# Attention scores on one Trainium2 core: the turned part as two fp32r products with split queries

## The chip, the cores and the metric

The kernel runs on one core of a Trainium2 chip. The metric is the time of one execution on the device in microseconds (us). A core has a matrix engine (TensorE, "PE" in the profile, with its weight loads as "PEld"), three engines for elementwise work (VectorE "DVE", ScalarE "ACT", GpSimd "POOL"), a SyncE queue ("SP") that starts transfers here, an on-chip memory SBUF of 128 partitions, and PSUM, into whose banks TensorE writes its products. Each engine works through a queue of its own and waits for others by semaphores.

## The reference

The program is a two-layer trunk over 256 positions of width 1024. Each layer is a feed-forward part, a mixer and another feed-forward part; the first layer's mixer is a convolution module, the second's is latent attention with 8 heads. The change touches the scores of that attention alone:

```python
q_nope, q_rope = q[..., :QK_NOPE], q[..., QK_NOPE:]          # 128 and 64 wide
q_rope = apply_rope(q_rope, cos[:, :, None, :], sin[:, :, None, :])
k_rope = apply_rope(k_rope, cos, sin)                         # one key for all heads
...
s = (jnp.einsum("bqhd,bkhd->bhqk", q_nope[:, q0:q1], k_nope[:, :q1],
                preferred_element_type=jnp.float32)
     + jnp.einsum("bqhr,bkr->bhqk", q_rope[:, q0:q1], k_rope[:, :q1],
                  preferred_element_type=jnp.float32)) * scale
mask = chunk_id[q0:q1, None] >= chunk_id[None, :q1]
s = jnp.where(mask[None, None], s, -jnp.inf)
p = jax.nn.softmax(s, axis=-1).astype(v.dtype)
outs.append(jnp.einsum("bhqk,bkhd->bqhd", p, v[:, :q1]))
```

Queries go in two blocks of 128; block 0 sees 128 keys, block 1 all 256. Within a block the mask lets a query see the chunks of 64 positions up to its own.

## The kernel before

**Number formats.** TensorE multiplies tiles declared fp32 in two recorded instructions per matmul and tiles declared fp32r (a rounded fp32) in one. Nearly all weight products of the kernel are therefore split: a weight is cast on ScalarE to an fp32r high part `hi` (L246), VectorE subtracts to get the low part `lo` (L247), and three fp32r products (`mm3`, L332, L335, L336) take the place of one fp32 product. Inside the attention, the scores and the value products are plain fp32.

**Where the scores get their operands.** `nope` (its eviction is L1522) projects the unturned queries `QN` and keys `KN`. The turned ("rope") queries of a block of 128 positions come as `qr`, are turned by VectorE in `rope` (L1407 to L1414, with scratch tiles of tag `rp512`), transposed on TensorE (L443, tile `tp`) four pairs of heads at a time, and copied out of PSUM into `QR` (recorded as L258, since the helper `urgent` wraps the call): the even heads, lying in partitions 0 to 63, by ScalarE, the odd heads, in partitions 64 to 127, by VectorE. `QR` has room for both parities, 128 partitions each; the 64 partitions that a parity doesn't use hold zeros and two rows of ones. `KR`, the turned key, is laid out the same way (L1554): the key in the half of its parity, and -1e30 in the two rows of the other half that meet the ones, which is how the mask is added by the product itself. GpSimd fills these constants at the start of the attention (L1432, L1437). The turned key is transposed with both halves alike, so each half of the 128 partitions holds the whole 64-wide key.

**The scores.** For each head `scores` takes one PSUM bank and, for both query blocks, adds an fp32 product of `QN` and `KN` (L1581) and one of `QR` and `KR` (L1582). `softmax` takes row maxima on VectorE (L1594, scaled in L1595), exponentials on ScalarE (L1597), reciprocal and scaling on VectorE (L1600, L1602). The probabilities are transposed (L443), copied by ScalarE (`ptT`, L1609), multiplied with the values `VV` (L1618, L1619), and the output is split by ScalarE and VectorE (L1613, L1614) for the output projection.

**Order.** Heads 0, 1 and 2 are scored first, then the unturned queries of the last four heads are projected (48 matmuls), then heads 3 to 7 follow one by one with the output projection's products between them. The values are projected (`v`, evicted in L1569 to `VV`) between the transposes of the queries and the first scores. Before the first exponential ScalarE loads its table, with a dummy exponential placed behind the last eviction of `VV`. A scheduler at build time settles the order in each engine's queue from priorities (`urgent` raises one) and from explicit `order` calls; on the chip the queues run as written. PSUM tiles of tag "B" share three banks in rotation: the transposed keys of the two blocks, the transposed queries of the two blocks and then the scores of heads 0, 1, 2 take them one after the other. A tile waits until the readers of the tile before it in the same bank are done.

Of the kernel before, what the change touches and what calls it, by code (L numbers as in the profile page):

```python
# [11 lines left out]
F32 = mybir.dt.float32  # L12
F32R = mybir.dt.float32r
# [6 lines left out]
P = 128  # L20
D = 1024
S = 256
# [5 lines left out]
CHUNK = 64  # L28
# [3 lines left out]
H = 8  # L32
# [57 lines left out]
def trunk(ctx: ExitStack, tc: tile.TileContext, x, xt, first, pos, invf, gfin, wdw,  # L90
          f1w13, f1w2, f2w13, f2w2, cw1, cw2, wa, wuq, wukv, wo, wpair, out):
    nc = tc.nc
# [12 lines left out]
    def uid(s):  # L105
        n_uid[0] += 1
        return f"{s}_{n_uid[0]}"
# [4 lines left out]
    def bank(tag, name):  # L112
        return ps.tile([P, 512], F32, tag=tag, name=uid(name), bufs=BANKS[tag])
# [40 lines left out]
    def order(ins, first):  # L154
        tc.add_manual_dep(ins.ins, first.name, mybir.DependencyInfo(
            mybir.DependencyClass.NoSync, mybir.DependencyReason.DATA), reason="order")
# [95 lines left out]
    def urgent(f):  # L252

        def g(*args, **kw):
            traced = nc.cur_bb.bb.instructions
            n = len(traced)
            with tc.high_priority():
                r = f(*args, **kw)  # L258
            last = {ins.engine: ins for ins in traced[n:]}
            for engine, ins in last.items():  # L260
                ahead_of.setdefault(engine, []).append(ins)
            return r
        return g
# [8 lines left out]
    def weights(n=1, more=True):  # L272
        out = []
        for _ in range(n):
            n_used[0] += 1
            if more:
                load_ahead()
            else:
                load_ahead(0)
            out.append(loaded[n_used[0] - 1])  # L280
        return out
# [48 lines left out]
    def mm3(o, ah, al, bh, bl, start, stop, after=(), seeded=False):  # L330

        mm = nc.tensor.matmul(o, ah, bl, start=start, stop=False, skip_group_check=seeded)  # L332
        for a in after:
            order(mm, a.ins)
        nc.tensor.matmul(o, ah, bh, start=False, stop=False, skip_group_check=seeded)  # L335
        return nc.tensor.matmul(o, al, bh, start=False, stop=stop, skip_group_check=seeded)  # L336
# [75 lines left out]
    def tbs(tb):  # L412
        return slice(tb * P, (tb + 1) * P)
# [26 lines left out]
    def transposed(src, q, n, after=(), turned=None):  # L440
        b = bank("B", "tp")
        for j in range(n):
            tp = nc.tensor.transpose(b[:, j * P:(j + 1) * P], src[:, (q + j) * P:(q + j + 1) * P], ident)  # L443
            if turned is not None:
                turned.append(tp)
            for a in after:
                order(tp, a.ins)
        return b
# [951 lines left out]
    def rope(pool, dst, src, n, cc, sn, tb, after=()):  # L1400

        w = n * 64
        t1, t2 = (pool.tile([P, w], F32, tag=f"rp{w}", name=uid("rp"), bufs=3 if n > 1 else 4) for _ in range(2))
        a = t1[:, :w].rearrange("p (n i f) -> p n i f", i=2, f=32)
        b = t2[:, :w].rearrange("p (n i f) -> p n i f", i=2, f=32)
        full = [P, n, 2, 32]
        turned = [nc.vector.tensor_tensor(a, src, cc[:, tb, :, :].unsqueeze(1).to_broadcast(full), op=ALU.mult)]  # L1407
        for i in range(2):
            turned.append(nc.vector.tensor_tensor(b[:, :, i, :], src[:, :, 1 - i, :],
                                                  sn[:, tb, i, :].unsqueeze(1).to_broadcast([P, n, 32]), op=ALU.mult))  # L1410
        for ins in turned:
            for first in after:
                order(ins, first.ins)
        nc.vector.tensor_add(dst, t1[:, :w], t2[:, :w])  # L1414


    def mla(X, make_next, cc, sn):
        with tc.tile_pool(name="mla", bufs=1) as act:
            return mla_in(act, X, make_next, cc, sn)

    def mla_in(act, X, make_next, cc, sn):
# [4 lines left out]
        CKl = act.tile([P, 2, S], F32R, tag="CKl", name="CKl")  # L1426


        KR = act.tile([P, 2, S], F32, tag="KR", name="KR")
        QR = act.tile([P, 2, H // 2, S], F32, tag="QR", name="QR")  # L1430
        for x, fill in ((KR, -1e30), (QR, 1.0)):
            nc.gpsimd.memset(x, 0.0)  # L1432
            for parity in range(2):
                for tb in range(NT):
                    row = 64 * (1 - parity) + 32 * tb
                    t = tb * P + (CHUNK if x is KR else 0)
                    nc.gpsimd.memset(x[row:row + 1, parity, ..., t:t + CHUNK], fill)  # L1437

        last_low = [None]

# [42 lines left out]
        last = None  # L1483
        for tb in range(NT):
# [5 lines left out]
            last = last_low[0]  # L1490
# [17 lines left out]
        KN = xp.tile([P, H, S], F32, tag="Xh", name="KN")  # L1508
        QN = xp.tile([P, H, S], F32, tag="Xl", name="QN")
        VV = act.tile([P, NT, H * VH], F32, tag="VV", name="VV")  # L1510

        def nope(part, dst, nk, ch, cl, width, h0, heads, after=()):

            hi, lo = part
            for i in range(heads[0], heads[1], 2):
                b = bank("A", "nope")
                for e in range(2):
                    for k in range(nk):
                        c = slice(k * width + (i + e) * P, k * width + (i + e + 1) * P)
                        mm = mm3(b[:, e * S:(e + 1) * S], hi[:, c], lo[:, c], ch[:, k, :], cl[:, k, :],  # L1520
                                 k == 0, k == nk - 1, after if k == 0 else ())
                nc.scalar.copy(dst[:, h0 + i:h0 + i + 2, :], b.rearrange("p (e t) -> p e t", t=S))  # L1522
            return mm
# [4 lines left out]
        for tb in range(NT):  # L1528
            u = bank("A", "qr")
            qu.append(u)  # L1530
            for k in range(4):
                after = (last,) if k == 0 else turned if (tb, k) == (0, 2) else ()
                last = mm3(u, CQh[:, k, tbs(tb)], CQl[:, k, tbs(tb)], hi[:, k * 512:(k + 1) * 512],
                           lo[:, k * 512:(k + 1) * 512], k == 0, k == 3, after)
# [14 lines left out]
        last = nope(part, QN, 4, CQh, CQl, 512, 0, (0, 4), turned)  # L1549
        for t in range(NT):  # L1550
            b = transposed(kd[t], 0, 1, (last,))
            for i in range(2):
                half = slice(64 * i, 64 * i + 64)
                nc.scalar.copy(KR[half, i, tbs(t)], b[half, :P])  # L1554
        for tb in range(NT):
            b = transposed(qr[tb], 0, 4, (last,)).rearrange("p (j t) -> p j t", t=P)
            for parity, copy in ((0, nc.scalar.copy), (1, nc.vector.tensor_copy)):
                half = slice(64 * parity, 64 * parity + 64)
                urgent(copy)(QR[half, parity, :, tbs(tb)], b[half])
        kpart, = weights()  # L1560
        nope(kpart, KN, 2, CKh, CKl, D, 0, (0, H))
        (hi, lo), = weights()
        for tb in range(NT):
            for d in range(2):
                b = bank("A", "v")
# [10 lines left out]
        def scores(hd):  # L1576
            b = bank("B", "sc")
            sc = {0: b[:, :P], 1: b[:, P:P + S]}
            for qb in range(NT):
                n = (qb + 1) * P  # L1580
                nc.tensor.matmul(sc[qb], QN[:, hd, tbs(qb)], KN[:, hd, :n], start=True, stop=False)  # L1581
                last = nc.tensor.matmul(sc[qb], QR[:, hd % 2, hd // 2, tbs(qb)], KR[:, hd % 2, :n], start=False,  # L1582
                                        stop=True)
            score_last.append(last)
            return softmax(sc)

        @urgent
        def softmax(sc):
            nm = small.tile([P, NT], F32, tag="nm", name=uid("nm"))
            sm = small.tile([P, NT], F32, tag="sm", name=uid("sm"))  # L1590
            pr = act.tile([P, 3 * P], F32, tag="pr", name=uid("pr"), bufs=3)
            pn = {0: pr[:, :P], 1: pr[:, P:]}
            for qb in range(NT):
                nc.vector.reduce_max(nm[:, qb:qb + 1], sc[qb], axis=AX.X)  # L1594
            maxima.append(nc.vector.tensor_scalar(nm, nm, -SCALE, None, op0=ALU.mult))  # L1595
            for qb in range(NT):
                last = nc.scalar.activation(pn[qb], sc[qb], AF.Exp, scale=SCALE, bias=nm[:, qb:qb + 1],  # L1597
                                            accum_out=sm[:, qb:qb + 1])
            powers.append(last)
            nc.vector.reciprocal(sm, sm)  # L1600
            for qb in range(NT):
                last = nc.vector.tensor_scalar(pn[qb], pn[qb], sm[:, qb:qb + 1], None, op0=ALU.mult)  # L1602
            scaled.append(last)
            return pr
# [22 lines left out]
        table = urgent(nc.scalar.activation)(small.tile([P, 1], F32, tag="silu", name="exp"), neghalf, AF.Exp)  # L1627
        order(table, kept.ins)
        pr[0] = scores(0)
        pr[1] = scores(1)  # L1630
        pr[2] = scores(2)

        for j, i, highs, lows in ((0, 0, None, maxima[2]), (0, 1, None, scaled[0]), (1, 0, powers[2], scaled[1]),
# [51 lines left out]
    class Rows512:  # L1685

        n = {"ht": 0, "hb": 0}
# [128 lines left out]
```

## Time and profile before

| | |
|---|---|
| runs | 896.81, 897.5, 900.43 us (median 897.5) |
| the profiled execution | 897.52 us, of which the span 895.7 us |
| TensorE busy | 887.9 us (99% of the span) |
| VectorE busy | 743.6 us (83%) |
| ScalarE busy | 571.8 us (64%) |
| attention, first scores to last output product | about 667 to 714 us of the span |
| score products (L1581, L1582) | 32 records each: 8 heads, 2 blocks, 2 records per fp32 matmul |

How to read the profile: times are from the span's start. In the timeline a row is start, duration, engine, line, operation, output<-inputs, shape and count; in brackets stands the idle time of the engine before it and what ended that. Consecutive equal instructions are merged into one row ("x4"). A TensorE record's duration includes the pipeline's fill and drain, so neighbouring records overlap and the cost of a matmul is read from start to start. The profile prints fp32r operands of TensorE as f32; which they are follows from the tiles. In the chain of waits a row is start, length, engine, tile and line of a piece of the chain that ended last.

### The profile page before, as it was taken

To read this page: it belongs to the slowest core of one execution; us is meant where nothing else is said; L and a number is where in the kernel's file an instruction comes from. 1 tells how busy PE (TensorE), PEld (TensorE's weight loads), DVE (VectorE), ACT (ScalarE), POOL (GpSimd) and SP (SyncE) were. 2 spreads that over 40 slices of the span, in tenths; PEclk is the share of its full clock that TensorE was granted. 3 is DMA by queue.
4 is the path that set the end of the run, shared out by engine and by line. 5 is a ranking of instruction groups with operands and counts; after the bars stand their busy time and mean duration, and the time that the engine had idled before them with its cause. 6 is when DMAs were issued, how large, how long until landed. Compare 5 with 4: busy or idle time off the path is not lost.

```text
span 895.7 us, 12244 instructions
## 1 busy us (share of the span) xinstructions
PE 887.9 (99%) x4221; PEld 745.7 (83%) x4221; DVE 743.6 (83%) x1083; ACT 571.8 (64%) x993; POOL 105.2 (12%) x227
## 2 busy tenths in 40 slices
PE   9999999999999999999999999999999999999997
PEld 7888888898988888888888888888899888888886
DVE  6787779579998999999598989995768579999973
ACT  7966458488876646656375566673677566474762
POOL 1000000079962000000010000001400010000000
PEclk9999999999999999999999999999999999999999
DMA  9997629834215864939759369396635449387551
GB/s 336 354 341 252 229 59 367 296 124 165 95 60 193 291 257 147 386 97 372 271 177 340 113 221 350 114 387 202 219 142 189 141 147 345 107 285 291 165 210 48
DMA packets 71054, 198.94 MB, mean 222 GB/s; under 512 B 12368, under 2 KB 41936, under 8 KB 51664
## 3 DMA queue, kind: packets, MB, share of 16 engines
q1 hardware_dynamic: 70560, 197.47, 61.9%
q8 instruction: 33, 0.54, 0.2%
q10 hardware_dynamic: 432, 0.69, 0.2%
q14 instruction: 29, 0.24, 0.1%
HBM read 181.87 MB, written 16.25 MB: 221 GB/s over the span
## 4 chain that ended last, share of the span: by engine, by line
PE 78%; DVE 10%; DMA 8%; issue 2%; SPq 1%; ACT 1%; POOL 0%; DVEq 0%; ACTq 0%
PE u L332 10%; PE u L336 10%; PE u L335 10%; PE o L336 9%; PE o L332 9%; PE o L335 9%; PE u L1002 3%; PE gate L1002 3%; DVE lo L247 3%; DMA gd<-gt 2%; PE u L408 2%; DVE lo L200 2%; DMA raw<-in_f2w 1%; DMA rows<-gd 1%; DMA hd<-rows 1%
## 5 line engine op out<-in xcount | busy, mean ns | idle before, releaser
L247 DVE TENSOR_TENSOR lo<-raw,hi 128x1024 fp32r<-128x1024 f32 (+1 forms) x236 | 276.0, 1210 | 39.0 <-ACT hi L246 37.7
L246 ACT CAST hi<-raw 128x1024 fp32r<-128x1024 f32 (+1 forms) x238 | 236.7, 1044 | 86.1 <-DMA raw<-in_f2w 28.0
L332 PE MATMUL u<-lo,Xh 128*128 128x512 f32 x612 | 238.7, 390 | 0.3
L335 PE MATMUL u<-hi,Xh 128*128 128x512 f32 x612 | 238.2, 389 | 0.0
L336 PE MATMUL u<-hi,Xl 128*128 128x512 f32 x612 | 237.9, 389 | 0.0
L332 PEld LDWEIGHTS u<-lo,Xh 128*128 128x128 f32 x612 | 114.9, 188 | 25.9 <-DVE lo L200 1.6
L336 PEld LDWEIGHTS u<-hi,Xl 128*128 128x128 f32 x612 | 114.9, 188 | 24.6 <-DVE Xl L462 0.5
L335 PEld LDWEIGHTS u<-hi,Xh 128*128 128x128 f32 x612 | 114.9, 188 | 23.7
L214 ACT CAST hi<-raw 128x1024 fp32r<-128x1024 f32 x98 | 97.6, 1049 | 54.2 <-DVE raw L200 47.5
L200 DVE TENSOR_TENSOR lo<-raw,hi 128x1024 fp32r<-128x1024 f32 x98 | 115.9, 1216 | 5.5 <-ACT hi L214 5.3
L332 PE MATMUL o<-lo,Gh 128*128 128x512 f32 (+1 forms) x276 | 106.6, 386 | 0.0
L335 PE MATMUL o<-hi,Gh 128*128 128x512 f32 (+1 forms) x276 | 106.5, 386 | 0.0
L336 PE MATMUL o<-hi,Gl 128*128 128x512 f32 (+1 forms) x276 | 106.5, 386 | 0.0
L434 POOL TENSOR_TENSOR ms<-ss 128x1 f32<-128x1 f32 x16 | 8.1, 511 | 598.2 <-ACT junk L426 598.2
L200 DVE TENSOR_TENSOR raw<-raw,raw 128x2048 f32<-128x2048 f32 x28 | 63.8, 2278 | 1.7 <-DMA raw<-in_f2w 1.4
L335 PEld LDWEIGHTS o<-hi,Gh 128*128 128x128 f32 x276 | 51.8, 188 | 10.5
L336 PEld LDWEIGHTS o<-hi,Gl 128*128 128x128 f32 x276 | 51.8, 188 | 10.5
L332 PEld LDWEIGHTS o<-lo,Gh 128*128 128x128 f32 x276 | 51.8, 188 | 10.4
L1091 DVE SCALAR_TENSOR_TENSOR acc<-V,dw,acc 128x128 f32<-128x128 f32 (+1 forms) x174 | 53.9, 389 | 0.0
L953 ACT ACTIVATE s<-u,R 128x512 f32<-128x512 f32 (+1 forms) x48 | 30.9, 647 | 26.9 <-PE u L336 26.2
L1112 ACT ACTIVATE prod<-V,dw 128x128 f32<-128x128 f32 (+1 forms) x128 | 45.8, 416 | 2.0 <-POOL Y L1113 1.0
L794 DVE SCALAR_TENSOR_TENSOR h<-o,rh,h 128x512 f32<-128x512 f32 (+1 forms) x18 | 12.9, 718 | 29.0 <-PE o L336 29.0
(265 smaller groups left out, 1260.2 us busy)
## 6 DMA issues: line engine op xcount, KB each, us to landing
raw<-in_f2w SPq DMA_DIRECT2D x66, 1024.0 KB, 6.5
raw<-in_f1w SPq DMA_DIRECT2D x62, 1024.0 KB, 6.6
raw<-in_cw SPq DMA_DIRECT2D x12, 1024.0 KB, 4.9
gd<-gt SPq DMA_DIRECT2D x160, 64.0 KB, 2.9
gb<-gd SPq DMA_DIRECT2D x24, 256.0 KB, 2.9
rows<-gd SPq DMA_DIRECT2D x16, 256.0 KB, 4.1
raw<-in_wo SPq DMA_DIRECT2D x4, 1024.0 KB, 4.9
hd<-rows SPq DMA_DIRECT2D x56, 64.0 KB, 2.4
```

Of the source, the lines that this page charges most:

```text
L200: ins = nc.vector.tensor_sub(out, left, right)
L214: casts[n, i] = nc.scalar.copy(hi[:, c], raw[:, c]), sub(lo[:, c], raw[:, c], hi[:, c].bitcast(F32))
L246: casts[len(loaded), i] = (nc.scalar.copy(hi[:, c], raw[:, c]), low.tensor_sub(lo[:, c], raw[:, c], hi[:, c].bitcast(F32)))
L247: low.tensor_sub(lo[:, c], raw[:, c], hi[:, c].bitcast(F32)))
L332: mm = nc.tensor.matmul(o, ah, bl, start=start, stop=False, skip_group_check=seeded)
L335: nc.tensor.matmul(o, ah, bh, start=False, stop=False, skip_group_check=seeded)
L336: return nc.tensor.matmul(o, al, bh, start=False, stop=stop, skip_group_check=seeded)
L408: mm = nc.tensor.matmul(o, al if kind == "x" else ah, bl if kind == "l" else bh, start=start and n == 0, stop=stop and n == len(kinds) - 1)
L953: nc.scalar.activation(s[:, :w], u[0, tb][:, :w], AF.Silu, scale=X.r[tb])
L1002: mm = nc.tensor.matmul(u[:, t], w[:, c], X.x[:, k, t], start=(k == 0), stop=(k == KT - 1))
L1091: dve_last.append(nc.vector.scalar_tensor_tensor(out if j == j1 - 1 else y, v, w, y, op0=ALU.mult, op1=ALU.add))
L1112: prods_last.append(nc.scalar.activation(p, v, AF.Copy, scale=w))
```

## The change

The turned product is split as the weight products are, but in two fp32r products instead of three. `KA` holds the high part of the key (fp32r) in both halves. `KR` now holds the low part of the key, with the mask rows as before; `QR` holds the high part of the queries with the rows of ones as before. A new tile `QA` per parity and block holds, one above the other, the high part of the queries in the half of their parity and their low part in the other half. So `QA` x `KA` gives high x high plus low x high in one product over all 128 partitions, and `QR` x `KR` gives high x low plus the mask. Low x low is dropped. `QN` x `KN` stays fp32.

The high parts of the queries are cast by ScalarE for both parities, VectorE subtracts for the low part and copies the high part into `QA`. The four `QA` tiles share tag `rp512` with the scratch of `rope`, which gets six buffers instead of three. The three products of block 1 are put in another order than those of block 0 (the fp32 product last), and explicit `order` calls fix the sequence within a head.

```diff
     def rope(pool, dst, src, n, cc, sn, tb, after=()):
...
-        t1, t2 = (pool.tile([P, w], F32, tag=f"rp{w}", name=uid("rp"), bufs=3 if n > 1 else 4) for _ in range(2))
+        t1, t2 = (pool.tile([P, w], F32, tag=f"rp{w}", name=uid("rp"), bufs=6 if n > 1 else 4) for _ in range(2))
...
-        KR = act.tile([P, 2, S], F32, tag="KR", name="KR")
-        QR = act.tile([P, 2, H // 2, S], F32, tag="QR", name="QR")
+        KA = act.tile([P, S], F32R, tag="KA", name="KA")
+        QA = {}
+        KR = act.tile([P, 2, S], F32R, tag="KR", name="KR")
+        QR = act.tile([P, 2, H // 2, S], F32R, tag="QR", name="QR")
         for x, fill in ((KR, -1e30), (QR, 1.0)):
-            nc.gpsimd.memset(x, 0.0)
+            nc.gpsimd.memset(x.bitcast(F32), 0.0)
...
         for t in range(NT):
             b = transposed(kd[t], 0, 1, (last,))
+            nc.scalar.copy(KA[:, tbs(t)], b[:, :P])
             for i in range(2):
                 half = slice(64 * i, 64 * i + 64)
-                nc.scalar.copy(KR[half, i, tbs(t)], b[half, :P])
+                nc.vector.tensor_sub(KR[half, i, tbs(t)], b[half, :P], KA[half, tbs(t)].bitcast(F32))
         for tb in range(NT):
             b = transposed(qr[tb], 0, 4, (last,)).rearrange("p (j t) -> p j t", t=P)
-            for parity, copy in ((0, nc.scalar.copy), (1, nc.vector.tensor_copy)):
-                half = slice(64 * parity, 64 * parity + 64)
-                urgent(copy)(QR[half, parity, :, tbs(tb)], b[half])
+            for parity in range(2):
+                half, rest = (slice(64 * i, 64 * i + 64) for i in (parity, 1 - parity))
+                high = QR[half, parity, :, tbs(tb)]
+                urgent(nc.scalar.copy)(high, b[half])
+                both = act.tile([P, 512], F32R, tag="rp512", name=uid("QA"), bufs=6).rearrange("p (j t) -> p j t", t=P)
+                urgent(nc.vector.tensor_sub)(both[rest], b[half], high.bitcast(F32))
+                urgent(nc.vector.tensor_copy)(both[half], high)
+                QA[parity, tb] = both
...
+            last = None
             for qb in range(NT):
                 n = (qb + 1) * P
-                nc.tensor.matmul(sc[qb], QN[:, hd, tbs(qb)], KN[:, hd, :n], start=True, stop=False)
-                last = nc.tensor.matmul(sc[qb], QR[:, hd % 2, hd // 2, tbs(qb)], KR[:, hd % 2, :n], start=False,
-                                        stop=True)
+                three = [(QN[:, hd, tbs(qb)], KN[:, hd, :n]), (QA[hd % 2, qb][:, hd // 2], KA[:, :n]),
+                         (QR[:, hd % 2, hd // 2, tbs(qb)], KR[:, hd % 2, :n])]
+                for i, (rows_of, keys) in enumerate(three if qb == 0 else three[1:] + three[:1]):
+                    mm = nc.tensor.matmul(sc[qb], rows_of, keys, start=i == 0, stop=i == 2)
+                    if last is not None:
+                        order(mm, last.ins)
+                    last = mm
```

More of the change, by code (lines that the diff above doesn't have):

```diff
@@ L1436, in mla_in @@
                     t = tb * P + (CHUNK if x is KR else 0)
-                    nc.gpsimd.memset(x[row:row + 1, parity, ..., t:t + CHUNK], fill)
+                    nc.gpsimd.memset(x[row:row + 1, parity, ..., t:t + CHUNK].bitcast(F32), fill)
         last_low = [None]
```

## The prediction

> **What bounds the kernel now.** I read the page first, then the chain of waits from the projections of the attention to the end, then the timeline of those 60 us engine by engine.
>
> ```profile
> PE 887.9 (99%) x4221; PEld 745.7 (83%) x4221; DVE 743.6 (83%) x1083; ACT 571.8 (64%) x993; POOL 105.2 (12%) x227
> ...
> PE 78%; DVE 10%; DMA 8%; issue 2%; SPq 1%; ACT 1%; POOL 0%; DVEq 0%; ACTq 0%
> ```
>
> TensorE is hardly ever without work, so a microsecond saved or lost on TensorE between the projections and the end of the attention moves everything behind it. Two things are to be read from the timeline: what a product costs from start to start (durations overlap), and how far the copies that feed the scores run ahead of them.
>
> **The change part by part.**
>
> *The price of a product.* Each fp32 matmul of the code is two records, each fp32r matmul one.
>
> ```profile
> 671.41 0.28 PE L335 MATMUL nope<-CQ,hi 128*128 128x256 f32 x1
> 671.53 0.28 PE L336 MATMUL nope<-CQ,lo 128*128 128x256 f32 x1
> ...
> 677.60 0.39 PE L1582 MATMUL sc<-KR,QR 128*128 128x128 f32 x2
> 677.82 0.60 PE L1581 MATMUL sc<-KN,QN 128*128 128x256 f32 x2
> 678.25 0.59 PE L1582 MATMUL sc<-KR,QR 128*128 128x256 f32 x2
> 678.69 0.49 PE L443 MATMUL tp<-ident,pr 128*128 128x128 f32 x3
> ```
>
> The columns are start and duration in us, engine, line and operation. From the chain of waits, which gives each piece its time on the chain:
>
> ```profile
> 665.70 0.44 PE tp L443 x4
> ```
>
> The turned fp32 product takes 677.82 - 677.60 = 0.22 us on 128 keys and 678.69 - 678.25 = 0.44 us on 256. An fp32r product on 256 columns takes 671.53 - 671.41 = 0.12 us. No row has an fp32r product on 128 columns. Its bounds are 0.06 us (half of the 256-column step) and 0.22 us (no better than fp32). I take 0.11 us, from the nearest row: the four one-record transposes with 128 columns and full weight loads take 0.44 us, 0.11 us each. Per head the change removes 0.22 + 0.44 = 0.66 us and adds 2 x 0.11 + 2 x 0.12 = 0.46 us: 0.20 us saved, over 8 heads -1.6 us (by the bounds between -2.4 us, with 0.06, and +0.2 us, with 0.22).
>
> The page "TensorE: Matmul & The Clock Gate" of the Trainium skill, section "Back-to-back issue gap", gives some 81 ns for a sustained load-and-multiply pair at 128 columns. By that figure the 16 short products would be an estimated 0.5 us cheaper together than by the row; no row of this case shows such a product, so the row's 0.11 us stands.
>
> *The keys.* ScalarE's four half copies become two full copies; VectorE gets four half subtractions.
>
> ```profile
> 655.70 1.08 ACT L1554 COPY KR<-tp 64x128 f32<-64x128 f32 x4
> ```
>
> ```profile
> 650.88 1.12 DVE L462 SCALAR_TENSOR_TENSOR CKl<-tp,G,CKh 128x128 fp32r<-128x128 f32 x4
> ```
>
> On ScalarE that is about half of 1.08 us, and on VectorE about 4 x 0.28 = 1.1 us. Both end before 662, five microseconds ahead of the scores, so I cost them at nothing. In the changed order VectorE turns the second queries half a microsecond earlier and does the key subtractions behind them. They also free the two PSUM banks of the keys only then, which the transposes and the first scores wait for, well in time. The fills on GpSimd are the same in number and size, and the queues of SyncE and GpSimd keep their order: zero.
>
> *The queries.* For each of the two token blocks there were one copy on ScalarE and one on VectorE. Now ScalarE makes both high parts, and VectorE a subtraction and a copy for each.
>
> VectorE's rows, then TensorE's, then ScalarE's:
>
> ```profile
> 662.28 0.69 DVE L258 COPY QR<-tp 64x512 f32<-64x512 f32 x1 [1.89 <-ACT QR L258]
> 666.83 0.69 DVE L258 COPY QR<-tp 64x512 f32<-64x512 f32 x1 [3.86 <-ACT QR L258]
> 669.75 1.15 DVE L1594 TENSOR_REDUCE nm<-sc 128x1 f32<-128x128 f32 x4 [2.23 <-PE sc L1582]
> 670.82 0.28 DVE L1595 TENSOR_SCALAR nm<-nm 128x2 f32<-128x2 f32 x2
> ...
> 672.23 1.22 DVE L247 TENSOR_TENSOR lo<-raw,hi 128x1024 fp32r<-128x1024 f32 x1
> 673.36 0.54 DVE L1602 TENSOR_SCALAR pr<-pr,sm 128x128 f32<-128x128 f32 x2
> ```
>
> ```profile
> 667.13 0.39 PE L336 MATMUL v<-hi,CKl 128*128 128x512 f32 x1
> 667.37 0.38 PE L1581 MATMUL sc<-KN,QN 128*128 128x128 f32 x2
> ...
> 669.98 0.38 PE L1581 MATMUL sc<-KN,QN 128*128 128x128 f32 x2
> ```
>
> ```profile
> 666.70 1.99 ACT L246 CAST hi<-raw 128x1024 fp32r<-128x1024 f32 x2
> 668.59 0.58 ACT L1569 COPY VV<-v 128x512 f32<-128x512 f32 x1
> 669.17 1.28 ACT L258 ACT_TABLE_LOAD   x1
> 670.47 0.20 ACT L258 ACTIVATE exp<-neghalf 128x1 f32<-128x1 f32 x1
> 671.01 0.37 ACT L1597 ACTIVATE pr<-sc,nm 128x128 f32<-128x128 f32 x1 [0.34 <-DVE nm L1595]
> ...
> 673.40 2.01 ACT L246 CAST hi<-raw 128x1024 fp32r<-128x1024 f32 x2
> 675.29 0.61 ACT L1522 COPY QN<-nope 128x512 f32<-128x512 f32 x1
> 677.25 0.59 ACT L1522 COPY QN<-nope 128x512 f32<-128x512 f32 x1 [1.34 <-PE nope L336]
> 677.73 0.48 ACT L1609 COPY ptT<-tp 128x384 f32<-128x384 f32 x1
> ```
>
> VectorE gains 4 x 0.69 for the subtractions and at most as much for the copies (the copy row is from PSUM; these read SBUF), less the two copies it had: about 4 us. By amount this fits into its 1.89 + 3.86 + 2.23 = 8.0 us of waiting. By place it does not. Three PSUM banks go round: keys 0 and 1, queries 0 and 1, scores of heads 0, 1, 2. Head 2's scores get the bank of query block 1, and so wait until its last reader is done. Before, that was the VectorE copy ending at 666.83 + 0.69 = 667.5, with TensorE arriving at 669.98: 2.5 us of room. In the changed program's order the fourth ScalarE copy (block 1, odd heads) stands behind the last copy of the values, the table load and the first exponential, and the subtraction that reads the bank comes after it. The second copy of a block also waits for the first one's subtraction; that costs nothing here, because block 0's is done by 666 beside the value products, and block 1's by 667.7, ahead of the load's end.
>
> So: the last value product still starts at 667.13 (the same products and transposes are ahead of it) and ends at 667.5. Behind it on ScalarE come the value copy 0.58, the table load 1.28, the exponential 0.20 and the fourth copy, which has a value copy's size per partition, 0.58: it ends at 670.2. With 0.69 for the subtraction the bank is free at 670.9. TensorE starts the scores at 667.37 and does, ahead of head 2, block 0 of heads 0 and 1 (2 x 0.44) and block 1 of head 0 (0.12 + 0.12 + 0.44): it is there at 668.9. (Head 0's block 1 needs the third pair of VectorE's steps, ready at about 668.4 where TensorE asks at 668.2; that 0.2 us is part of the stop.) It stands still for 2.0 us in all. Bounds: 0.5 us, if load and exponential held nothing up (1.48 less), and 2.2 us with some 0.1 us for each of two hand-overs. Behind that product on TensorE's queue stand the projection of the last four heads and all scores: all of it moves.
>
> *The softmax behind it.* VectorE now takes the first maxima after the last query copy, not at 669.75 but at 670.9 + 0.6 = 671.5. In the new order: maxima of head 0 (half of 1.15) to 672.1, their scaling to 672.2, its two exponentials (673.40 - 671.01 = 2.4 for three heads, 0.8 each) to 673.0, reciprocal and scaling of the probabilities to 673.8, a weight subtraction (1.15) to 675.0, the maxima of heads 1 and 2 (1.15) to 676.1 and 0.28 to 676.4, their exponentials (1.6) to 678.0, a weight cast (2.0) to 680.0, a projection copy (0.6) to 680.6, and only then the copy of head 0's turned probabilities (0.48): 681.1. The value product of head 0 needs that one. TensorE, after its stop at 670.9, does the rest of head 2 (0.44 + 0.68), the projection (48 x 0.12 = 5.8) with head 1's second block in it (0.68), a transposition (0.33), head 3 (1.12) and another transposition: it is there at 680.2 and stands 0.9 us. Before, that copy came at 677.73, ready when wanted. Bounds: 0 (if the casts take turns otherwise) and 1.2 us.
>
> *Sum.* -1.6 + 2.0 + 0.9 = +1.3 us at the output projection, where later heads find all ready again. The work behind is the same program in the same order and with the same waits.
>
> ```profile
> 703.78 0.42 DVE L1614 TENSOR_TENSOR Ol<-pv,Oh 128x256 fp32r<-128x256 f32 x1 [3.32 <-ACT Oh L1613]
> ```
>
> ```profile
> 713.12 0.45 PE tp L443 x4
> ```
>
> VectorE waits again at 703.78, so its 5 us of extra work are paid off by then. The chain into the last feed-forward part starts from TensorE's transposes at 713.12, so the 1.3 us goes through whole. The profiled execution took 897.52 us, 1.8 us of it outside the span, and the runs' median is 897.5: I say 898.8.
>
> **The rivals.**
>
> A. *The stops do not happen, and it gets faster*: if the fourth copy slips in ahead of the table load's end in effect, or the bank is free earlier, the 1.6 us stays: 895.9. For it speaks VectorE's 8.0 us of waiting, against it that ScalarE does its queue in order (at 668.59 a value copy starts that had been ready at 667.5, behind two casts). It decides below 1.6 us of stops in all. Chance 0.13.
>
> B. *fp32r on 128 columns is no cheaper than fp32* (the change's promise half broken): products +0.2 instead of -1.6 us. The first heads' part falls into the stops (some 0.3 + 0.4 us less waiting): +0.2 + 1.6 + 0.5 = +2.3 us, 899.8. Chance 0.17.
>
> C. *The late start collides in the last part*, where feed-forward turns go through DRAM beside weight loads:
>
> ```profile
> 749.62 4.89 DMA rows<-gd
> ```
>
> ```profile
> 767.48 2.88 DMA rows<-gd
> ```
>
> One such transfer took 2.0 us more than another. One or two of them hit anew give +1.3 + 2 to 4: 900.8 to 902.8. They can as well be missed (-0.7: 896.8). Chance 0.08 and 0.04.
>
> D. *The short product costs its lower bound*, 0.06 us: 0.8 us less TensorE work, half of it lost again in the stops: 898.4. For it speaks that streaming 128 columns is half of 256, against it the transposes' 0.11 us. It never decides. The skill's 81 ns would lie between this and the forecast. Chance 0.08.
>
> **How the numbers follow.** Forecast 0.50, A 0.13, B 0.17, C 0.12, D 0.08. The forecast alone spans 898.0 to 899.8. With A at the lower end, and B and the nearer half of C at the upper, the range is 895.9 to 901.2. The bound of 0.5%, about what a measurement of this kernel can tell from no change (its runs lie between 896.81 and 900.43), is 893.0 to 902.0: every case but the far half of C lies within it. Faster 0.02, within 0.92, slower 0.06.
>
> **What would show it.** Right: a TensorE gap of about 2 us ahead of the first product of head 2, released by a VectorE subtraction into QA, with the table load between value copy and fourth QR copy on ScalarE; a second gap near 681 ahead of the first value product, released by the probabilities' copy; KA,QA products of one record each, 0.11 and 0.12 us from start to start. Wrong: KA,QA on 128 columns in two records or steps of 0.2 us; no idle TensorE between 668 and 682; TensorE's transposes of the last rows at other than 1.3 us later; or a last part of another length.

## The result

The changed kernel takes 900.22 us (median of 12 runs, 898.92 to 902.6) against 897.68 us for the kernel before on the same chip (12 runs): a ratio of 1.0027, with a 95% interval of 1.0019 to 1.0036. The ratio leaves out one run of before that took 989.38 us. The changed kernel is slower, but by less than 0.5%. The profiled execution took 900.88 us, with a span of 899.1 us (before: 897.52 and 895.7).

The page of the changed kernel, its busy times and the engines' shares of the chain that ended last:

```profile
PE 887.4 (99%) x4221; PEld 744.3 (83%) x4221; DVE 748.8 (83%) x1093; ACT 572.1 (64%) x993; POOL 105.5 (12%) x227
...
PE 77%; DVE 9%; DMA 8%; issue 2%; ACT 2%; SPq 1%; POOL 0%; DVEq 0%; ACTq 0%
```

TensorE issues as many records as before (32 one-record products replace 16 two-record ones) and is busy 0.5 us less, VectorE 5.2 us more with ten more instructions. In the chain, TensorE and VectorE each lost a point and ScalarE gained one. ScalarE's work came into the chain in two places, and the timeline of TensorE shows both as idle time. (Columns: start and duration in us, engine, line, operation; in brackets the idle time ahead and what ended it.)

```profile
668.42 0.39 PE L336 MATMUL v<-hi,CKl 128*128 128x512 f32 x1
668.64 0.38 PE L1596 MATMUL sc<-KN,QN 128*128 128x128 f32 x2
...
669.83 0.59 PE L1596 MATMUL sc<-KN,QN 128*128 128x256 f32 x2
672.40 0.46 PE L1596 MATMUL sc<-KN,QN 128*128 128x128 f32 x2 [1.99 <-DVE QA L258]
...
680.34 0.39 PE L1596 MATMUL sc<-KN,QN 128*128 128x128 f32 x2
680.48 0.31 PE L1596 MATMUL sc<-KA,QA 128*128 128x128 f32 x1
680.62 0.27 PE L1596 MATMUL sc<-KR,QR 128*128 128x128 f32 x1
680.73 0.33 PE L1596 MATMUL sc<-KA,QA 128*128 128x256 f32 x1
680.90 0.28 PE L1596 MATMUL sc<-KR,QR 128*128 128x256 f32 x1
681.02 0.60 PE L1596 MATMUL sc<-KN,QN 128*128 128x256 f32 x2
681.46 0.49 PE L443 MATMUL tp<-ident,pr 128*128 128x128 f32 x3
682.34 0.70 PE L1634 MATMUL pv<-ptT,VV 128*128 128x256 f32 x2 [0.39 <-ACT ptT L1625]
```

A head (680.34 to 681.46) now takes 1.12 us. Before it took 0.22 us on 128 keys and 0.44 us on 256 for each of its two fp32 products, 1.32 us. That is the saving. (Within the head the starts don't step evenly: 0.14, 0.14, 0.11, 0.17, 0.12 and 0.44 us. Their sum is what counts.) The first stop stands ahead of head 2's first product. The product before it starts at 669.83 and holds TensorE for 0.43 us (the step of 256 columns), so TensorE could have gone on at 670.26: it stood for 2.14 us. The second stands ahead of the first value product: three transposes take 0.33 us from 681.46, and the product starts at 682.34, 0.55 us later.

The chain of waits of the changed kernel says what was late (start, length, engine, tile, line):

```profile
668.84 0.59 ACT VV L1580
669.43 1.28 ACT L258
...
670.95 0.59 ACT QR L258
671.57 0.70 DVE QA L258
672.40 1.35 PE sc L1596 x8
...
677.33 0.44 ACT QN L1527
677.81 1.73 ACT pr L1613 x8
679.54 1.88 ACT hi L246 x2
681.42 0.49 ACT QN L1527
681.90 0.39 ACT ptT L1625
682.34 0.70 PE pv L1634 x2
...
715.88 0.45 PE tp L443 x4
...
893.11 0.49 DVE h L794
```

The first group is ScalarE's queue: last value copy, table load (1.28), a 0.20 us exponential, the fourth query copy; then VectorE's subtraction, the last reader of the PSUM bank. The second group is ScalarE's queue again: a copy of projected queries that had waited for TensorE, the exponentials of heads 1 and 2, two weight casts and two copies, all ahead of TensorE's first value product. In the chain of before, TensorE ran through both places without a break.

To see how much of the 3.4 us between the two spans belongs to the change, I cut the span at two VectorE instructions that both kernels have: the last scaling into `cn` ahead of the projections, and the first addition of the attention's output to `h` (L789). Between them lies everything that the change touches. The timelines' rows, first of before, then of the changed kernel:

```profile
647.08 0.47 DVE L1465 TENSOR_SCALAR cn<-a,rr 128x256 f32<-128x256 f32 x1
711.79 2.06 DVE L789 TENSOR_TENSOR h<-o,h 128x512 f32<-128x512 f32 x3 [0.79 <-PE o L336]
```

```profile
648.33 0.48 DVE L1470 TENSOR_SCALAR cn<-a,rr 128x256 f32<-128x256 f32 x1
714.55 2.05 DVE L789 TENSOR_TENSOR h<-o,h 128x512 f32<-128x512 f32 x3 [0.79 <-PE o L336]
```

The attention grew from 64.71 to 66.22 us, by 1.51 us. Another 1.25 us came ahead of it, in instructions that stand in the same order in both kernels, and 0.62 us behind it, up to the last addition to `h` (889.73 us before, 893.11 us in the chain above). The experiments take these pieces apart. All kernels by the same two cuts, from one profiled execution each, in us:

| kernel | ahead | attention | behind, to the last addition |
|---|---|---|---|
| before | 647.08 | 64.71 | 177.94 |
| before, profiled anew | 646.89 | 64.72 | 178.85 |
| before with early transposes | 647.45 | 65.10 | 179.57 |
| changed | 648.33 | 66.22 | 178.56 |
| changed, measured anew | 647.41 | 66.17 | 177.91 |
| table load last | 646.72 | 65.81 | 177.89 |
| early transposes, even heads first | 648.26 | 64.56 | 178.08 |
| early transposes, odd heads first | 647.63 | 63.95 | 177.90 |
| copies only, fp32 products | 646.88 | 67.20 | 177.96 |

### The profile page after: what moved, and what is told of

Same layout as the page of the kernel before. It is cut to its first block, busy times and chain, and to the rows that moved or that the text cites. A ratio compares the mean times of both kernels' runs of the same rounds, so it can differ in the third digit from the quotient of the medians.

```text
span 899.1 us, 12257 instructions
## 1 busy us (share of the span) xinstructions
PE 887.4 (99%) x4221; PEld 744.3 (83%) x4221; DVE 748.8 (83%) x1093; ACT 572.1 (64%) x993; POOL 105.5 (12%) x227
## 4 chain that ended last, share of the span: by engine, by line
PE 77%; DVE 9%; DMA 8%; issue 2%; ACT 2%; SPq 1%; POOL 0%; DVEq 0%; ACTq 0%
PE u L332 10%; PE u L336 10%; PE u L335 10%; PE o L336 9%; PE o L335 9%; PE o L332 9%; PE u L1002 3%; PE gate L1002 3%; PE u L408 2%; DMA gd<-gt 2%; DVE lo L247 2%; DMA raw<-in_f2w 2%; DVE lo L200 1%; DMA hd<-rows 1%; DMA rows<-gd 1%
```

## The experiments

### The changed kernel again, and the kernel before again

No edit: which pieces of the difference come back?

> The changed kernel once more, for a second trace of it. In the first one the attention took 1.5 us more than in the trace of before (the late part of the difference 2.76 us at its end less 1.25 us at its start), 1.25 us of difference stood already ahead of the changed code and 0.6 us arose behind it. If the two outer pieces are chance, they come out otherwise here (anything between -1 and +1.5 us each) and the attention's 1.5 us comes out again within 0.2 us. If the change causes them (by where tiles lie, say), all three come out again.

> The kernel before once more, for a second trace: attention segment 64.7 us again within 0.2 us; the parts ahead of and behind it may move by up to 1 us if they are chance.

The changed kernel took 899.53 us against 898.44 us (ratio 1.0013, 1.0004 to 1.0021). Its attention took 66.17 us, 1.46 us more than before, with both stops again (the timeline of TensorE in that run):

```profile
671.50 0.46 PE L1596 MATMUL sc<-KN,QN 128*128 128x128 f32 x2 [1.99 <-DVE QA L258]
...
681.42 0.70 PE L1634 MATMUL pv<-ptT,VV 128*128 128x256 f32 x2 [0.39 <-ACT ptT L1625]
```

The part ahead was now only 0.33 us longer than in the first profile of before, and the part behind as long as there. The kernel before, profiled anew (898.23 us), had an attention of 64.72 us, the same to 0.01, but a part behind that was 0.91 us longer. So the attention's 1.5 us is the change; the outer 1.9 us of the first pair did not come back, and the unchanged program varies from one execution to the next too. Two measurements of the same pair gave 2.5 and 1.1 us, with intervals of 1.7 to 3.2 and 0.4 to 1.9 us (the ratios' bounds times the time of before). The attention's 1.5 us lies between the two and only in the second interval; why the first pair lies further apart is not shown.

### The table load behind the fourth query copy

If the load on ScalarE's queue makes the first stop, moving it behind the copy must shrink that stop (run table_last). In the trace the load and the exponential behind it are the only ones that changed places with another instruction on TensorE, VectorE, ScalarE and GpSimd: the fourth copy now runs ahead of them.

```diff
-                urgent(nc.scalar.copy)(high, b[half])
+                high_copy = urgent(nc.scalar.copy)(high, b[half])
...
-        order(table, kept.ins)
+        order(table, high_copy.ins)
```

> The exponential's table load is put behind the fourth ScalarE copy of the queries, and nothing else. Theory (the bank of query block 1 is what head 2 waits for, and the table load delays its last reader): the stop ahead of head 2 falls from 2.0 us to about 0.5 us. But the second stop, ahead of the first value product, is set by the softmax chain of heads 0 to 2 on VectorE and ScalarE, which ends at the same time, so it grows from 0.55 us to about 1.8 us: total 0.2 to 0.3 us faster than the changed kernel. Rival (the stop has another cause, such as the load of the keys' low part): the first stop stays at 2.0 us. Second rival (the second stop is only an echo of the first): both shrink, 1.5 us faster or more.

899.25 us against 898.44 us (ratio 1.0013, 1.0004 to 1.0022). TensorE's two stops:

```profile
669.30 0.46 PE L1596 MATMUL sc<-KN,QN 128*128 128x128 f32 x2 [0.48 <-DVE QA L258]
...
680.37 0.70 PE L1634 MATMUL pv<-ptT,VV 128*128 128x256 f32 x2 [1.54 <-ACT ptT L1625]
```

The first stop fell from 1.99 to 0.48 us of idle time, by the load and the exponential (1.48 us) to within 0.03: what held the bank is shown. But the second grew from 0.39 to 1.54 us, and the attention became only 0.4 us shorter. Counted from the end of the transposes, as in the result, it is 1.70 us, where 1.8 was expected. TensorE arrives earlier at the first value product, while the copy of the turned probabilities comes only 0.4 us earlier, behind the same casts on ScalarE. Two casts earlier in that queue (669.85, 1.98 us) now hold up head 0's exponentials until 671.85, though its maxima were ready at 670.47. Each stop hides part of the other.

### Early transposes, odd heads first

To remove the stops and keep the products (run early_turn): the transposes of the two query blocks are held ahead of the first and of the second group of `v`'s products (in the trace at 661.55 and 663.36 us; in the changed kernel they stand at 664.08 and 667.05), the odd heads' pair of each block comes first, and the table load is last as above.

```diff
+        tps = []
         for tb in range(NT):
-            b = transposed(qr[tb], 0, 4, (last,)).rearrange("p (j t) -> p j t", t=P)
-            for parity in range(2):
+            b = transposed(qr[tb], 0, 4, (last,), tps).rearrange("p (j t) -> p j t", t=P)
+            for parity in (1, 0):
...
-                    mm3(b, CKh[:, k, tbs(tb)], CKl[:, k, tbs(tb)], hi[:, c], lo[:, c], k == 0, k == 1)
+                    mm3(b, CKh[:, k, tbs(tb)], CKl[:, k, tbs(tb)], hi[:, c], lo[:, c], k == 0, k == 1,
+                        tps[3:4] if (tb, d, k) == (0, 0, 0) else tps[7:] if (tb, d, k) == (0, 1, 0) else ())
```

> As table_last, and the two transposes of the queries are held ahead of the first and the second group of value products (instead of wherever the scheduler put them), and the odd heads' operands are made before the even ones. Theory: everything that reads the bank of query block 1 is done by 668, no TensorE stop ahead of head 2 at all; the maxima of the first three heads come two us earlier, and the second stop shrinks to some 0.6 us. Attention then takes -1.6 + 0.6 = 1.0 us less than in the kernel before, 2.3 to 2.5 us less than in the changed one. Rival (the products themselves, not the stops, cost the time): no faster than the changed kernel by more than 0.5 us.

896.99 us against 898.44 us for the kernel before (ratio 0.9989, 0.9980 to 0.9998) and 899.53 us for the changed one on the same chip: the fastest of all, though its gain on the kernel before is small. The first stop is gone: TensorE shows no idle time from 664 us to the first value product. Of the second this row is left:

```profile
679.41 0.70 PE L1636 MATMUL pv<-ptT,VV 128*128 128x256 f32 x2 [0.46 <-ACT ptT L1627]
```

The attention takes 63.95 us, 0.76 us less than before and 2.27 us less than in the changed kernel. With the stops mostly gone, about half of the products' 1.6 us shows as a gain; the second stop takes at least 0.46 us of the rest. What is left of it waits no longer for the casts: ScalarE stands idle for 0.92 us until TensorE's transposes give it the probabilities to copy.

### The same with even heads first

The run even_first changes one line of early_turn:

```diff
-            for parity in (1, 0):
+            for parity in range(2):
```

> early_turn with the even heads' operands made first, as in the changed kernel; transposes and table load stay early. Theory (the second stop hangs on the order in which the softmax of heads 0 to 2 gets through VectorE and ScalarE, not on the bank): no stop ahead of head 2, but a stop of about 1.5 us ahead of the first value product, so the attention takes 1.0 us more than in early_turn and about as long as in the kernel before. Rival (early transposes alone make the difference): as early_turn within 0.2 us.

898.09 us against 897.63 us (ratio 1.0002, 0.9991 to 1.0012): no difference from before. The attention takes 64.56 us, 0.61 us longer than with odd heads first, and the idle time ahead of the first value product is the place:

```profile
680.67 0.70 PE L1636 MATMUL pv<-ptT,VV 128*128 128x256 f32 x2 [1.10 <-ACT ptT L1627]
```

1.10 against 0.46 us is 0.64 us. I had expected 1.0. The scheduler made other orders with it. Here a projection copy on ScalarE (674.95 us, after 1.75 us of waiting for TensorE) stands between the exponentials of head 0 and those of heads 1 and 2, and two weight casts behind them. With odd heads first the exponentials of all three heads run one after the other from 672.59 us. The pair that comes first may act through this order alone; the runs don't separate the two.

### The early transposes in the kernel before

Is the gain of the early transposes the change's products, or something that the kernel before could have had as well?

```diff
+        tps = []
...
-            b = transposed(qr[tb], 0, 4, (last,)).rearrange("p (j t) -> p j t", t=P)
+            b = transposed(qr[tb], 0, 4, (last,), tps).rearrange("p (j t) -> p j t", t=P)
...
-                    mm3(b, CKh[:, k, tbs(tb)], CKl[:, k, tbs(tb)], hi[:, c], lo[:, c], k == 0, k == 1)
+                    mm3(b, CKh[:, k, tbs(tb)], CKl[:, k, tbs(tb)], hi[:, c], lo[:, c], k == 0, k == 1,
+                        tps[3:4] if (tb, d, k) == (0, 0, 0) else tps[7:] if (tb, d, k) == (0, 1, 0) else ())
```

> The kernel before (fp32 products, no split) with only the two transposes of the queries held ahead of the first and second group of value products. Theory (what early_turn gains over before is the fp32r products' price, and before had no stop to remove): no gain, 0 to 0.5 us slower in the attention. Rival (the earlier transposes are worth something by themselves): 0.5 to 1 us faster.

897.78 us against 897.63 us (ratio 0.9996, 0.9988 to 1.0005), with an attention of 65.10 us, 0.39 us longer than before. Up to the first value product nothing moved: it starts 31.92 us behind the `cn` scaling (679.37 - 647.45), before 31.93. The 0.39 us arises behind it, where the scheduler also put the products of the output projection in another order. So the early transposes alone gain nothing where nothing waited for them, which fits the gain above being the products' price. What the table load's place would do in the fp32 kernel was not tried.

### The copies without the cheaper products

All of the change's preparation, but every score product in fp32, and without the product that adds the mask (run copies_only).

```diff
-        KA = act.tile([P, S], F32R, tag="KA", name="KA")
-        KR = act.tile([P, 2, S], F32R, tag="KR", name="KR")
-        QR = act.tile([P, 2, H // 2, S], F32R, tag="QR", name="QR")
+        KA = act.tile([P, S], F32, tag="KA", name="KA")
+        KR = act.tile([P, 2, S], F32, tag="KR", name="KR")
+        QR = act.tile([P, 2, H // 2, S], F32, tag="QR", name="QR")
...
-                both = act.tile([P, 512], F32R, tag="rp512", name=uid("QA"), bufs=6).rearrange("p (j t) -> p j t", t=P)
+                both = act.tile([P, 512], F32, tag="rp512", name=uid("QA"), bufs=6).rearrange("p (j t) -> p j t", t=P)
...
-                three = [(QN[:, hd, tbs(qb)], KN[:, hd, :n]), (QA[hd % 2, qb][:, hd // 2], KA[:, :n]),
-                         (QR[:, hd % 2, hd // 2, tbs(qb)], KR[:, hd % 2, :n])]
+                three = [(QN[:, hd, tbs(qb)], KN[:, hd, :n]), (QA[hd % 2, qb][:, hd // 2], KA[:, :n])]
```

> All steps of the changed kernel that make KA, KR, QR and QA, in its order, but the four tiles declared fp32 and the scores made of two fp32 products per block as before (QN with KN, QA with KA). The product that adds the mask is left out, so the softmax runs over all keys. Products at the price of before, stops of the changed kernel. Theory: stops of 1.8 and 0.5 us (less than in the changed kernel, since TensorE comes later to the second one), nothing gained: +1.9 us in the attention against before, 0.4 to 0.5 us slower than the changed kernel. Rival (the fp32r products of 128 columns cost what fp32 ones do): the same time per head as the changed kernel, 1.12 us; by the theory 1.32 us per head.

900.25 us against 898.44 us (ratio 1.0020, 1.0010 to 1.0030). TensorE's stops, and head 3:

```profile
670.96 0.46 PE L1595 MATMUL sc<-KN,QN 128*128 128x128 f32 x2 [1.79 <-DVE QA L258]
...
679.28 0.39 PE L1595 MATMUL sc<-KN,QN 128*128 128x128 f32 x2
679.51 0.82 PE L1595 MATMUL sc<-KA,QA 128*128 128x128 f32 x4
680.17 0.59 PE L1595 MATMUL sc<-KN,QN 128*128 128x256 f32 x2
680.60 0.49 PE L443 MATMUL tp<-ident,pr 128*128 128x128 f32 x3
681.28 0.70 PE L1633 MATMUL pv<-ptT,VV 128*128 128x256 f32 x2 [0.19 <-ACT ptT L1624]
```

The head costs 680.60 - 679.28 = 1.32 us, as before the change, and both stops are there, so the preparation alone makes them. The attention is 2.49 us longer than before, more than the 1.9 us I had expected, and 0.98 us longer than in the changed kernel, where I had expected 0.4 to 0.5. The stops, counted from the end of the product ahead, are 1.96 and 0.35 us, which is nearly the whole 2.49. Together they are 2.31 us, as expected (1.8 and 0.5). My total of 1.9 us was less than its own stops.

### Eight more short products per head

The price of an fp32r product on few columns was the term without a row. Eight more products of `QA` and `KA` in block 0, on 128 keys for heads 0 to 3 and on 64 keys for heads 4 to 7:

```diff
                     last = mm
+                    if qb == 0 and i == 1:
+                        wide = 128 if hd < 4 else 64
+                        for _ in range(8):
+                            mm = nc.tensor.matmul(sc[qb][:, :wide], rows_of, keys[:, :wide], start=False, stop=False)
+                            order(mm, last.ins)
+                            last = mm
```

> The changed kernel with eight more products of QA with KA in block 0 of each head, on 128 keys for heads 0 to 3 and on 64 keys for heads 4 to 7, into the same sums (so the high part counts nine times there). It measures the price that the prediction had to bound. If the weight load sets it, both forms step by 0.11 us; if the stream sets it, 0.06 and 0.03 us; if fp32r on few columns costs what fp32 does, 0.22 us on 128.

One execution was profiled, of 904.92 us. Its timeline has a block of each width (the duration covers all eight):

```profile
681.30 1.06 PE L1603 MATMUL sc<-KA,QA 128*128 128x128 f32 x8
...
684.30 1.03 PE L1603 MATMUL sc<-KA,QA 128*128 128x64 f32 x8
```

And the groups by tile (minimum, median and maximum of one in ns) have the weight loads that stand beside them:

```profile
L1603 PEld LDWEIGHTS sc<-KA,QA x64: 188/192/192, 668.6 to 698.8; 128*128 128x128 f32 x64
```

The block ends one record's duration (0.27 and 0.28 us) after its last start, so seven steps take 1.06 - 0.27 and 1.03 - 0.28: 0.113 and 0.107 us each. Half the columns save at most 0.006 us. The step is not set by the columns streamed; what is equal in both is the instruction itself and its load of 128 x 128 weights. That the load sets the step is the reading that fits, not something these runs separate further.

The run also says what sets the first stop. Two of these blocks stand ahead of head 2, so TensorE comes there later, and its idle time falls from 1.99 to 0.26 us; but head 2 starts 24.09 us behind the `cn` scaling (672.18 - 648.09), as in the changed kernel (672.40 - 648.33 = 24.07). The bank sets that start, not TensorE's work ahead of it.

## Why the prediction was right

**Direction and size.** Forecast was 898.8 us, 1.3 us over the profiled execution of before, from a range of 895.9 to 901.2 and with 0.92 for a change of under 0.5%. The attention grew by 1.5 us in both profiles of the changed kernel, and the two measurements gave 2.5 and 1.1 us. The mechanism is the forecast's, the closeness is partly luck. The terms were off by +0.14, -0.35 and +0.4 us (below) and cancel in part. The first measurement, 900.22 us, lies above the 898.0 to 899.8 that the forecast alone spans, in the part of the range that was there for rivals B and C; the second, 899.53, lies inside.

**The price of a product.** Right: 0.20 us per head saved, as taken. The unseen term, the fp32r product on 128 keys, was taken as 0.11 us from the transposes and measured 0.11 us. That ends rival B (0.22 us, no cheaper than fp32) and rival D (0.06 us). The page "TensorE: Matmul & The Clock Gate" of the Trainium skill, section "Back-to-back issue gap", gives about 81 ns at 128 columns; this case's products step by 0.11 us, so the measurement decides against that figure here.

**The first stop.** Right in place, cause and size: released by the VectorE subtraction into `QA`, 2.14 us where 2.0 was taken, with TensorE arriving 0.1 us later than said (670.26, or 21.93 us behind the `cn` scaling; forecast 668.9, or 21.82). The forecast had the bank free 23.82 us behind that scaling (670.9 - 647.08); it was 23.94 (671.57 + 0.70 - 648.33). TensorE then restarted 0.14 us later (672.40), which the bounds' hand-over allowed for and the value taken did not. Rival A, in which the copy gets by ahead of the load, did not happen; moving the load behind the copy took 1.5 us off this stop.

**The second stop.** Right in place and cause, too large in size: 0.55 us measured, 0.9 taken. The value product started 34.01 us behind the scaling, where the forecast's 681.1 is 34.02; the copy's end was right to 0.1 us (681.90 + 0.39 = 682.29, or 33.96). The path to it was in part another. The forecast's sum runs over VectorE's maxima of heads 1 and 2, ready at 676.4, or 29.32; they were, at 677.70, or 29.37 (677.41 + 0.29 in VectorE's timeline). But in the trace's chain it is the copy of projected queries at 677.33 on ScalarE that stands ahead of these heads' exponentials, and the sum doesn't have that copy. Both were done within 0.1 us of each other. The difference in size is TensorE's side, which arrived at 681.46 + 0.33 = 681.79, 33.46 us behind the scaling instead of 33.12; 0.25 us of that is the later restart after the first stop (672.40, or 24.07, instead of 23.82).

**The sum.** -1.6 + 2.14 + 0.55 = 1.1 us of the 1.5 measured. Of the other 0.4 us, less than half lies ahead of the first value product: from the first score to it TensorE took 13.70 us (682.34 - 668.64) instead of 11.64, 2.06 more, where the saving of four heads and the two stops make 1.89. The rest lies behind: from there to the first transpose of `h` it took 33.38 us instead of 33.95, 0.57 less, where four heads make 0.8. About 0.1 us of this is the restart itself: the value product behind the second stop takes 0.53 us to the next one (682.34 to 682.87), the one at 686.39 takes 0.43. The steps are too small to show as idle rows, and the scheduler put some of the later products in another order. "Where later heads find all ready again" was not quite so; what makes the remainder stays open.

**VectorE's work.** Its copy `QA` from `QR` takes 0.42 us, not up to 0.69, and the key subtractions were done long before the scores at 668.64, as said:

```profile
661.43 1.21 DVE L1560 TENSOR_TENSOR KR<-tp,KA 64x128 fp32r<-64x128 f32 x4
...
671.57 0.69 DVE L258 TENSOR_TENSOR QA<-tp,QR 64x512 fp32r<-64x512 f32 x1 [2.14 <-ACT QR L258]
672.29 0.42 DVE L258 CAST QA<-QR 64x512 fp32r<-64x512 f32 x1
```

The 2.14 us that VectorE itself waits ahead of the subtraction shows that it was never the limit there: ScalarE's queue was.

**The late start in the last part** (rival C). The part behind was 177.91 and 178.56 us in the two profiles of the changed kernel and 177.94 and 178.85 us in two of the unchanged one. The transposes at the end of the attention came 2.76 us later (715.88 - 713.12), not 1.3, but 1.25 us of that stood ahead of the attention. In the first profile of the changed kernel the transfer of 4.89 us that the rival names did take longer, 6.01 us (at 752.44). But the last part was as short as before in the second profile, and it was longest, 179.57 us, in the fp32 kernel with early transposes, where that transfer took 5.41 us. Nothing ties a longer last part to the change.

## What to carry to other kernels

Cheaper products gain only what their operands' preparation leaves: ask which instruction reads a PSUM bank last, on which engine's queue it stands and what is ahead of it there. A queue that is 64% busy can still hold the bound, if a table load stands in the wrong place. And where several waits lie one behind another, taking away one moves TensorE to the next: here 1.5 us off the first stop was worth 0.4 us, until the preparation as a whole came earlier.

## What was not expected of the hardware

A product on 64 columns stepped by 0.107 us, as good as one on 128 (0.113 us), with a full weight load for each. And parts of the program that are the same instructions in the same order took up to 1.6 us more or less from one execution to another: 177.94 and 178.85 us behind the attention in two profiles of the kernel before, 646.7 to 648.3 us ahead of it over all profiles. On TensorE, 0.8 of the first pair's extra 1.25 us ahead arose between 275 and 287 us, where the chain of before runs through transfers (2.71 us at 274.61, 5.23 us at 283.43); what causes it was not tried.
